# Low halves of the w_out weights by accumulating DMAs instead of VectorE subtractions

## The chip, the cores and the metric

The kernel runs on one core of one Trainium2 chip. The metric is the device time of one execution in microseconds (us), lower is better. The core's engines are named as the profile names them: PE (TensorE, matmuls), DVE (VectorE), ACT (ScalarE), POOL (GpSimd) and SP (SyncE, which here only issues DMAs). The engines run their own instruction queues in order and wait for each other by semaphores; 16 DMA engines move the data of all queues.

## What is computed

One decoder layer for 512 positions and a model width of 2048. A conditioning vector c gives shift, scale and gate by an adaLN product; h is x scaled and shifted; one input product makes q, k, v, two gates and the two halves of a GLU; the attention branch (sliding window, 16 heads) and the convolution branch (depthwise convolution, layer norm, pointwise product) make 1024 channels each; the output product w_out mixes both, and a layer norm over the residual ends it.

```python
mod = (c_act @ w_ada[l] + b_ada[l])[:, None, :]
shift, scale, gate = jnp.split(mod, 3, axis=-1)
h = x * (1.0 + scale) + shift
proj = h @ w_in[l]
...
y_attn = banded_sink_attention(q, k, v, rel_bias, sinks[l]) * jax.nn.silu(g_attn)
y_conv = conformer_conv(...) * jax.nn.silu(g_conv)
y = jnp.concatenate([y_attn, y_conv], axis=-1) @ w_out[l]
x = layer_norm(ALPHA * x + gate * y, ln_g[l], ln_b[l])
```

## The kernel before

Every product is made of three passes on PE. Each float32 operand is split into a high half (rounded to the matmul's input format, `fp32r`) and a low half (what the rounding left), and `mm3` sums high x high, low x high and high x low in PSUM. For weights the split is made on the fly: `load_w` loads a block of 128 x 1024 values (512 KB) into a tile `wr`, ACT copies it into `wh` (the rounding, line 174), and DVE subtracts `wh` from `wr` into `wl` (line 175). The tiles `wr`, `wh` and `wl` have three buffers each.

The work runs in phases: (1) h and the GLU projections; (2) q, k, v, gate and attention, with the depthwise convolution as filling work on DVE; (3) the convolution's gate; (4) from about 545 to 632 us, the output product over the attention channels: 4 column groups n of 4 blocks of w_out, kp = 0 to 3, 24 matmuls a block (4 position tiles x 2 chunks x 3 passes); (5) the pointwise product w_pw, 8 blocks; (6) the output product over the convolution's channels, kp = 4 to 7. In phase 6 the column groups n = 0 and 1 take 8 blocks of w_out through `wh` and `wl` as in phase 4; the 8 blocks of n = 2 and 3 (the "late" blocks, `late_block`) are split meanwhile into the space of h (`hh`, `hl`), and a last product over them follows, one position tile after the other, with the layer norm behind each. The raw tiles of both kinds are the three buffers of `wr`.

Phase 4 has filling work on DVE: `gate_steps` streams the gate's part of w_ada through two buffers `wa` (32 half rows of 512 KB) and reduces each against the activations of c (`junk`, line 588). Its result is needed for the residual in phase 5.

The program's text gives what depends on what; the order within each engine's queue is set by a scheduler that places instructions by a model of their durations. A change of one instruction's kind can so move others.

Names used below: `wr`, `wh`, `wl` raw, high and low weights; `hh`, `hl` high and low halves of h, later of the attention's and the convolution's channels and of the late weights; `ych`, `ycl` the halves of the convolution branch; `prj`, `att` the two sets of PSUM tiles; `xs` tiles of x for the residual; `lg`, `lb` the layer norm's parameters; `z` the residual sum.

Of the kernel before, what the change touches and what calls it, by code (L numbers as in the profile page):

```python
# [10 lines left out]
F32 = mybir.dt.float32  # L11
# [33 lines left out]

# smalls: columns of one [128, n] array
SM_ADA = 0
# [6 lines left out]

# the first phase goes over the contraction chunks as they come; these pairs of
# output tiles (glu_a, glu_b) stay in PSUM, the others are summed part by part.
N_FIXED = 3
# [3 lines left out]

# microseconds of other work for the vector engine with each block of weights
N_WARM = 5
# [11 lines left out]
def plan():  # L75
    """The order of the first phase: the next chunk of h, unless the tensor engine would wait for weights."""
    done = {i: 0 for i in range(N_FIXED, NC8)}
    items, fixed, n_h = [("h", 0)], 0, 1
    dma, pe = 8.5, 11.0
    while n_h < NK:  # L80
        item = None
        i = min(done, key=lambda j: (done[j], j))
        n = min(n_h - done[i], PART[1])
        if pe - dma < LEAD:
            if fixed < n_h:
                item, dma, pe = ("fix", fixed), dma + 1.1, max(pe, dma + 2) + 3.9
                fixed += 1
            elif n >= min(PART[0], n_h):
                item, dma, pe = ("rot", i, done[i], n), dma + 0.37 * n, max(pe, dma + 2) + 1.3 * n
                done[i] += n  # L90
        if item is None:
            item, dma = ("h", n_h), dma + 6.6
            n_h += 1
        items.append(item)
    items += [("fix", k) for k in range(fixed, NK)]
    # what is left of each pair, most of it first
    rest = sorted(done, key=lambda j: (done[j], j))
    return items + [("rot", i, done[i], NK - done[i]) for i in rest if done[i] < NK]


def parts_of(k0, n):
    """At most four chunks to a block."""
    m = -(-n // 4)
    cuts = [k0 + n * a // m for a in range(m + 1)]
    return list(zip(cuts[:-1], cuts[1:]))


def w_in_blocks():
    """The blocks of w_in in the order of use: (first chunk, chunks, columns)."""
    blocks = []  # L110
    for item in plan():
        if item[0] == "fix":
            blocks.append((item, item[1], 1, [c for i in range(N_FIXED) for c in ab_cols(i)]))
        elif item[0] == "rot":
            for ka, kb in parts_of(*item[2:]):
                blocks.append((("rot", item[1], ka), ka, kb - ka, ab_cols(item[1])))
    for c in [C_K, C_V] + [x + 256 * j for j in range(NKV) for x in (0, C_GA)] + [C_GC + 256 * j for j in range(4)]:
        for k in range(0, NK, 4):
            blocks.append((("col", c, k), k, 4, [(c, 256)]))
    return blocks  # L120


def bucket_runs():
    """(bucket, first distance, one past the last distance) for distances 0..127."""
    max_exact = N_BUCKETS // 2
    runs = []
    for d in range(P):
        if d < max_exact:
            b = d
        else:  # L130
            big = np.log(np.float32(d) / np.float32(max_exact)) / np.float32(math.log(MAX_DISTANCE / max_exact))
            b = min(max_exact + int(np.float32(big * np.float32(N_BUCKETS - max_exact))), N_BUCKETS - 1)
        if runs and runs[-1][0] == b:
            runs[-1][2] = d + 1
        else:
            runs.append([b, d, d + 1])
    return runs


def build(tc, xT, x, c, wadaT, smalls, win, wpw, wout, relT, sinks, ln_g, ln_b, out):  # L140
# [11 lines left out]

    # ---- the activations of c, on all partitions
    ones = pp.tile([P, P], F32, name="ones")
# [17 lines left out]
    def split(raw, hi, lo, hi_engine=None):  # L172
        """hi + lo = raw, each with 12 significant bits."""
        nc.scalar.activation(hi, raw, AF.Copy)  # L174
        nc.vector.tensor_tensor(lo, raw, hi.bitcast(F32), op=ALU.subtract)  # L175
# [15 lines left out]
    def silu_c(pool, psp, tag):  # L191
        # the products of ones that come first set the tensor engine's clock
        warm = psp.tile([P, S], F32, name="warm", tag=tag)
# [5 lines left out]
        parts = [slice(i * S, (i + 1) * S) for i in range(4)]  # L199
        # the halves of c lie where the last chunks of h come later  # L200
        chl = [(hh[0:1, NK - 4 + i, :], hl[0:1, NK - 4 + i, :]) for i in range(4)]
# [12 lines left out]
    def ada(pool, cb, js, parts=1):  # L214
        """columns js of mod: for each, 128 outputs of the adaLN product, one per partition."""
        wa = [pool.tile([P, D], F32, name="wa", bufs=WA_BUFS) for j in js]
# [9 lines left out]

    # ---- phase 1: h and the GLU projections, chunk by chunk
    glu = {}
# [55 lines left out]
    def conv_steps():  # L284
        """the depthwise convolution, two chains at a time"""
        for i0 in range(0, NC8, 2):
# [14 lines left out]
    def take(gen, budget):  # L301
        """some of the work that fills the vector engine between the splits of the weights"""
        while budget > 0:
            cost = next(gen, None)
            if cost is None:
                return
            budget -= cost
# [9 lines left out]

    # ---- phase 2: q, k, v, the gate, and attention
    def chain(*gens):
# [10 lines left out]

    # the negated bias of each head over the distance + 128; elsewhere the mask
    rel = p2.tile([16, N_BUCKETS], F32, name="rel", bufs=1)
# [58 lines left out]
    def attention(j, qs, sg, nb, n):  # L391
        """a block of queries of four heads, in three stages"""
        blk = slice(n * P, (n + 1) * P)
# [6 lines left out]
        def scores():  # L400
            # the negated scores, and after them the negated sink
            e = kept["e"] = p2.tile([P, GRP, 2 * P + 1], F32, name="e")
# [36 lines left out]
        def values():  # L439
            pv = ps2.tile([P, S], F32, name="att", bufs=5)  # L440
            for half, (pth, ptl) in enumerate(kept["p"]):
# [3 lines left out]
                nc.tensor.matmul(pv[:HD, :], v[:, 0, :], ptl, start=False, stop=half == nh - 1, skip_group_check=True)  # L445
            # the products with the low halves of the values lie in the upper partitions
            low = p2.tile([HD, S], F32, name="low", bufs=1)
# [9 lines left out]

    # the stages of attention go between the products of the next projections
    stages = {}
# [7 lines left out]
    for j in range(NKV):  # L467
# [14 lines left out]
        nb = p2.tile([P, GRP, 256], F32, name="nb")  # L482
        # [query, head, 255 - key]
        nc.sync.dma_start(nb, bass.AP(tensor=ext_d.tensor, offset=ext_d.offset + GRP * j * 384 + 1,
# [7 lines left out]

    # ---- phase 3: the gate of the convolution, and its layer norm
    def gc_out(j):
# [26 lines left out]
    def norm_steps():  # L521
# [27 lines left out]
        ps = colsum(tot)  # L549
        # 1 / sqrt(var + eps), and one Newton step: r (1.5 - 0.5 v r^2)  # L550
        nc.scalar.activation(tot, ps, AF.Sqrt, bias=eps, scale=1.0 / D_CONV)
# [12 lines left out]
        yield None  # L564
        # the normalised channels, through silu, take the place of the last chunks of h
        for i in range(NC8):
# [33 lines left out]
    def y_split(k0):  # L600
        # y of attention takes the place of the first chunks of h
        if k0 < 8:
            for k in range(k0, k0 + 4):
                split(y[:, k, :], hh[:, k, :], hl[:, k, :])
# [5 lines left out]

    # ---- phase 4: the output product over the channels of attention
    def w_out_block(n, kp):
        return load_w(wout, (n * 8 + kp) * P * 1024, 1024)

# [20 lines left out]

    # ---- phase 5: the pointwise product, its bias and gate; the attention half so far into the residual
    p5 = es.enter_context(tc.tile_pool(name="p5", bufs=1, reuse_waits="tile"))
# [56 lines left out]

    # ---- phase 6: the output product over the channels of the convolution, and the last layer norm
    def yh(k):
# [12 lines left out]

    # the weights of the last two column groups take the place of h  # L710
    def late_block(n, kp):
# [3 lines left out]
        ks = slice((n - 2) * 8 + 2 * (kp - 4), (n - 2) * 8 + 2 * (kp - 4) + 2)  # L715
        split(raw.rearrange("p (a b) -> p a b", a=2), hh[:, ks, :], hl[:, ks, :])

# [13 lines left out]
    for t in range(NB):  # L731
        ts_ = slice(t * P, (t + 1) * P)
        for n in (2, 3):
            # the last product in two parts, for what follows it to start early
            parts = [slice(0, HALF), slice(HALF, S)] if (t, n) == (NB - 1, 3) else [slice(0, S)]
# [21 lines left out]
def laid_out(x, c, w_ada, b_ada, w_in, rel_bias, sinks, conv_w, conv_b, conv_ln_g, conv_ln_b, w_pw, b_pw, w_out,  # L757
             ln_g, ln_b):
    x, w_in = np.asarray(x)[0], np.asarray(w_in)[0]
    cols = lambda v, n: np.asarray(v)[0].reshape(n, P).T  # noqa: E731  # L760
    cw = np.asarray(conv_w)[0].T.reshape(NC8, P, TAPS).transpose(1, 0, 2).reshape(P, NC8 * TAPS)
# [31 lines left out]
```

## Time and profile before

| | |
|---|---|
| median of 3 runs | 790.63 us (789.19 to 792.8) |
| span of the profiled execution | 788.9 us |
| PE busy | 760.9 us, 96% |
| DVE busy | 676.0 us, 86% |
| ACT busy | 341.8 us, 43% |
| POOL busy | 20.5 us, 3% |
| 512 KB loads of w_out | 32, median 4.6 us from issue to landing |

The profile is of one execution. A busy PE is the sum of its matmuls' records; the records overlap, so that the distance from one matmul's start to the next tells the pace. The time before the first and after the last recorded instruction is not in the span; beside the median of the runs it is 1.7 us.

### The profile page before, as it was taken

How to read it: one execution, taken by the hardware profiler on the slowest of the kernel's cores; microseconds unless marked ns; L12 is line 12 of the kernel's file. 1: busy time of each engine (PE TensorE's matmuls, PEld its weight loads, DVE VectorE, ACT ScalarE, POOL GpSimd, SP SyncE). 2: the span in 40 equal slices, each digit the busy share in tenths (PEclk: the TensorE clock that was granted, in tenths of full speed). 3: DMA queues.
4: the chain of work that ended last, by engine and by line, in shares of the span. 5: the costliest groups of instructions: out<-in, count | busy, mean ns of one | idle time of the engine just before them, and what ended most of it. 6: DMA issues, size and time to landing. Idle time of an engine off the chain costs nothing.

```text
span 788.9 us, 9718 instructions
## 1 busy us (share of the span) xinstructions
PE 760.9 (96%) x3522; PEld 628.9 (80%) x3522; DVE 676.0 (86%) x1101; ACT 341.8 (43%) x574; POOL 20.5 (3%) x30
## 2 busy tenths in 40 slices
PE   5999999999999999999999999999999799999994
PEld 4787888878898888888888888888878588888883
DVE  6888988959999999999999998579795539877797
ACT  4543333333242346656756756445473145433000
POOL 0000000000230000000000100000000000000000
PEclk9999999999999999999999999999999989999997
DMA  8999988513332232322321322367667633684033
GB/s 308 414 412 410 359 324 308 185 60 109 114 134 101 86 104 95 107 67 78 107 81 54 106 81 81 102 225 222 239 215 243 221 134 123 224 302 152 0 107 107
DMA packets 39089, 136.10 MB, mean 173 GB/s; under 512 B 4337, under 2 KB 6785, under 8 KB 34817
## 3 DMA queue, kind: packets, MB, share of 16 engines
q1 hardware_dynamic: 39042, 135.49, 49.2%
q8 instruction: 27, 0.44, 0.2%
q14 instruction: 20, 0.16, 0.1%
HBM read 131.26 MB, written 4.22 MB: 172 GB/s over the span
## 4 chain that ended last, share of the span: by engine, by line
PE 80%; DVE 9%; DMA 7%; issue 2%; ACT 0%; SPq 0%; DVEq 0%
PE prj L187 14%; PE prj L188 14%; PE prj L189 14%; DMA wa<-in_wadaT 6%; PE rot L187 5%; PE rot L189 5%; PE rot L188 5%; PE att L188 4%; PE att L189 4%; PE att L187 4%; PE fix L187 3%; DVE junk L588 3%; PE fix L188 3%; PE fix L189 3%; PE att L433 2%
## 5 line engine op out<-in xcount | busy, mean ns | idle before, releaser
L174 ACT ACTIVATE wh<-wr 128x1024 fp32r<-128x1024 f32 (+2 forms) x129 | 127.3, 997 | 203.5 <-PE prj L188 109.7
L187 PE MATMUL prj<-hh,wh 128*128 128x512 f32 x480 | 188.5, 393 | 0.0
L189 PE MATMUL prj<-hh,wl 128*128 128x512 f32 x480 | 187.6, 392 | 0.0
L188 PE MATMUL prj<-hl,wh 128*128 128x512 f32 x480 | 187.5, 391 | 0.0
L175 DVE TENSOR_TENSOR wl<-wr,wh 128x1024 fp32r<-128x1024 f32 (+2 forms) x129 | 147.3, 1145 | 27.5 <-ACT wh L174 27.1
L295 DVE SCALAR_TENSOR_TENSOR cv<-u,sm,cv 128x512 f32<-128x512 f32 x240 | 169.5, 743 | 0.8
L189 PEld LDWEIGHTS prj<-hh,wl 128*128 128x128 f32 x480 | 90.2, 188 | 19.4 <-issue 0.2
L187 PEld LDWEIGHTS prj<-hh,wh 128*128 128x128 f32 x480 | 90.2, 188 | 18.8 <-issue 0.2
L188 PEld LDWEIGHTS prj<-hl,wh 128*128 128x128 f32 x480 | 90.3, 188 | 18.1
L224 DVE CUSTOM_DVE_ANT_0 junk<-wa,cb,sm 128x2048 bf16<-128x2048 f32 (+1 forms) x32 | 72.9, 2279 | 2.6 <-DMA wa<-in_wadaT 2.6
L187 PE MATMUL rot<-hh,wh 128*128 128x512 f32 x160 | 62.2, 393 | 1.7 <-DVE acc L272 1.7
L188 PE MATMUL rot<-hl,wh 128*128 128x512 f32 x160 | 62.6, 391 | 0.0
L189 PE MATMUL rot<-hh,wl 128*128 128x512 f32 x160 | 62.5, 392 | 0.0
L188 PE MATMUL att<-wl,hh 128*128 128x512 f32 (+1 forms) x144 | 50.9, 354 | 6.7 <-DVE wl L175 6.7
L189 PE MATMUL att<-wh,hl 128*128 128x512 f32 (+1 forms) x144 | 50.2, 349 | 0.0
L187 PE MATMUL att<-wh,hh 128*128 128x512 f32 (+1 forms) x144 | 48.5, 349 | 0.0
L188 PE MATMUL fix<-hl,wh 128*128 128x512 f32 x96 | 38.2, 398 | 0.0
L187 PEld LDWEIGHTS rot<-hh,wh 128*128 128x128 f32 x160 | 30.3, 189 | 9.5 <-DVE acc L272 1.7
L189 PE MATMUL fix<-hh,wl 128*128 128x512 f32 x96 | 37.8, 394 | 0.0
L188 PEld LDWEIGHTS att<-wl,hh 128*128 128x128 f32 x144 | 28.0, 194 | 11.9 <-DVE wl L175 8.6
L189 PEld LDWEIGHTS rot<-hh,wl 128*128 128x128 f32 x160 | 30.1, 188 | 6.8 <-DVE wl L175 0.3
L188 PEld LDWEIGHTS rot<-hl,wh 128*128 128x128 f32 x160 | 30.1, 188 | 6.4
(163 smaller groups left out, 1179.3 us busy)
## 6 DMA issues: line engine op xcount, KB each, us to landing
wr<-in_win SPq DMA_DIRECT2D x68, 512.0 KB, 3.4
wa<-in_wadaT SPq DMA_DIRECT2D x30, 1024.0 KB, 8.6
wa<-in_wadaT SPq DMA_DIRECT2D x36, 512.0 KB, 5.0
wr<-in_wout SPq DMA_DIRECT2D x32, 512.0 KB, 4.6
wr<-in_win SPq DMA_DIRECT2D x24, 384.0 KB, 9.0
xt<-in_xT SPq DMA_DIRECT2D x16, 256.0 KB, 9.1
wr<-in_wpw SPq DMA_DIRECT2D x8, 512.0 KB, 3.3
xs<-in_x SPq DMA_DIRECT2D x16, 256.0 KB, 5.2
```

What stands on the lines that cost most here:

```text
L174: nc.scalar.activation(hi, raw, AF.Copy)
L175: nc.vector.tensor_tensor(lo, raw, hi.bitcast(F32), op=ALU.subtract)
L187: nc.tensor.matmul(ps, lh, rh, start=start, stop=False)
L188: nc.tensor.matmul(ps, lh, rl, start=False, stop=False)
L189: nc.tensor.matmul(ps, ll, rh, start=False, stop=stop)
L224: nc.vector.tensor_tensor_reduce(junk[:, part], w[:, part], cb[:, part], 1.0, first, ALU.mult, ALU.add, mod[:, j:j + 1])
L295: nc.vector.scalar_tensor_tensor(cv[i][:, :S], glu[i][:, j:j + S], w, cv[i][:, :S], op0=ALU.mult, op1=ALU.add)
L433: nc.tensor.transpose(pt[:, hd * P:(hd + 1) * P], kept["e"][:, hd, half * P:(half + 1) * P], ident)
L588: nc.vector.tensor_tensor_reduce(junk, wa, cb[:, hs], 1.0, dst if half else first, ALU.mult, ALU.add, dst)
```

## The change

The low half of a w_out block is no longer a DVE subtraction. ACT writes the negated high half into the low tile (a copy with scale -1, rounded as the high half is), and then a DMA issued from POOL with `accum_op=add` adds the raw weights to it in place: -hi + raw. ACT writes the high half by a copy of its own as before. For the 16 blocks of phase 4 (kp < 4) the DMA reads the weights in HBM a second time, for the 16 blocks of phase 6 it reads the tile `wr`. The splits of w_in, w_pw and of activations are as they were. The diff also drops comments, which moves line numbers.

```diff
+    def add_raw(lo, src):
+
+        nc.gpsimd.dma_start(lo, src, accum_op=ALU.add)
+
     def w_out_block(n, kp):
-        return load_w(wout, (n * 8 + kp) * P * 1024, 1024)
+        src = wout[(n * 8 + kp) * P * 1024:][:P * 1024].rearrange("(p e) -> p e", p=P)
+        raw = wp.tile([P, 1024], F32, name="wr")
+        nc.sync.dma_start(raw, src)
+        hi = wp.tile([P, 1024], F32R, name="wh")
+        lo = wp.tile([P, 1024], F32R, name="wl")
+        nc.scalar.activation(lo, raw, AF.Copy, scale=-1.0)
+        add_raw(lo, src if kp < 4 else raw)
+        nc.scalar.activation(hi, raw, AF.Copy)
+        return hi, lo
...
     def late_block(n, kp):
         raw = wp.tile([P, 1024], F32, name="wr")
         off = (n * 8 + kp) * P * 1024
         nc.sync.dma_start(raw, wout[off:off + P * 1024].rearrange("(p e) -> p e", p=P))
         ks = slice((n - 2) * 8 + 2 * (kp - 4), (n - 2) * 8 + 2 * (kp - 4) + 2)
-        split(raw.rearrange("p (a b) -> p a b", a=2), hh[:, ks, :], hl[:, ks, :])
+        raw2 = raw.rearrange("p (a b) -> p a b", a=2)
+        nc.scalar.activation(hl[:, ks, :], raw2, AF.Copy, scale=-1.0)
+        add_raw(hl[:, ks, :], raw2)
+        nc.scalar.activation(hh[:, ks, :], raw2, AF.Copy)
```

The order of the queues changes with it, at three places that matter below. The first is DVE at the end of phase 4, before; `junk_5340`, `junk_5344` and `junk_5348` are the last three of the 32 half reductions, `wl_5241` and `wl_5279` the low halves of the last two w_out blocks, `wl_5364` and `wl_5417` those of the first two w_pw blocks.

```order
L588 ISA junk_5340,mod_65<-wa_5338,cb_4869,mod_65 128x1024
L588 ISA mod_65 128x1
L588 ISA junk_5344,mod_65<-wa_5342,cb_4869,sm_64 128x1024
L588 ISA mod_65 128x1
L175 TENSOR_TENSOR wl_5241<-wr_5238,wh_5240 128x1024
L588 ISA junk_5348,mod_65<-wa_5346,cb_4869,mod_65 128x1024
L588 ISA mod_65 128x1
L656 SCALAR_TENSOR_TENSOR dl_5393<-ident_70,mod_65,dh_5392 128x128 x4
L175 TENSOR_TENSOR wl_5279<-wr_5276,wh_5278 128x1024
L175 TENSOR_TENSOR wl_5364<-wr_5361,wh_5363 128x1024
L175 TENSOR_TENSOR wl_5417<-wr_5414,wh_5416 128x1024
```

The same place of DVE with the change; here `junk_5356`, `junk_5360` and `junk_5364` are the last three half reductions, `wl_5380` and `wl_5433` the low halves of the first two w_pw blocks.

```order
L588 ISA junk_5356,mod_65<-wa_5354,cb_4874,mod_65 128x1024
L588 ISA mod_65 128x1
L175 TENSOR_TENSOR wl_5380<-wr_5377,wh_5379 128x1024
L588 ISA junk_5360,mod_65<-wa_5358,cb_4874,sm_64 128x1024
L588 ISA mod_65 128x1
L588 ISA junk_5364,mod_65<-wa_5362,cb_4874,mod_65 128x1024
L588 ISA mod_65 128x1
L175 TENSOR_TENSOR wl_5433<-wr_5430,wh_5432 128x1024
```

The w_out splits are gone from between the reductions, and the first split of w_pw now stands ahead of the last two reductions, behind thirty.

The second place is SP in phase 6, before: the loads of the raw tiles and of x around the middle of the phase (`wr` of line 714 is a late block, of line 180 one that is used at once).

```order
L714 DMA wr<-in_wout 128x1024
L180 DMA wr<-in_wout 128x1024
L714 DMA wr<-in_wout 128x1024
L180 DMA wr<-in_wout 128x1024
L666 DMA xs<-in_x 128x512 x2
L693 DMA lb<-in_ln_b 128x2048
L666 DMA xs<-in_x 128x512 x8
L714 DMA wr<-in_wout 128x1024
```

The same place of SP with the change (late blocks at line 726, the others at line 619).

```order
L726 DMA wr<-in_wout 128x1024
L619 DMA wr<-in_wout 128x1024
L678 DMA xs<-in_x 128x512 x2
L705 DMA lb<-in_ln_b 128x2048
L678 DMA xs<-in_x 128x512 x7
L726 DMA wr<-in_wout 128x1024
L619 DMA wr<-in_wout 128x1024
L678 DMA xs<-in_x 128x512
```

The batch of x loads moves ahead of the third late block and the fourth of the others, which now wait for adds: each load of a raw tile into a buffer waits for the add that reads the buffer's former contents.

The third place is PE in phase 6 with the change, at the sixth block that is used at once (`wh_5989`, `wl_5990`); `att_6115` is a PSUM tile of the last product, `hh_71` and `hl_72` hold the late weights.

```order
L187 MATMUL att_5950<-wh_5989,ych_5371 128x512
L187 MATMUL att_6115<-hh_71,ych_5371 128x512
L188 MATMUL att_6115<-hl_72,ych_5371 128x512
L189 MATMUL att_6115<-hh_71,ycl_5372 128x512
L187 MATMUL att_6115<-hh_71,ych_5371 128x512
L188 MATMUL att_6115<-hl_72,ych_5371 128x512
L189 MATMUL att_6115<-hh_71,ycl_5372 128x512
L187 MATMUL att_6115<-hh_71,ych_5371 128x512
L188 MATMUL att_6115<-hl_72,ych_5371 128x512
L189 MATMUL att_6115<-hh_71,ycl_5372 128x512
L187 MATMUL att_6115<-hh_71,ych_5371 128x512
L188 MATMUL att_6115<-hl_72,ych_5371 128x512
```

Eleven matmuls of the last product stand there ahead of the first one that reads `wl_5990`; at the fifth, seventh and eighth of these blocks it is three each. Before, none of the last product's matmuls stood among these blocks.

## Rows read from the trace of the kernel before

**Rows 1.** The page: busy time by engine, and the clock granted in 40 slices.

```profile
PE 760.9 (96%) x3522; PEld 628.9 (80%) x3522; DVE 676.0 (86%) x1101; ACT 341.8 (43%) x574; POOL 20.5 (3%) x30
PE   5999999999999999999999999999999799999994
PEclk9999999999999999999999999999999989999997
```

**Rows 2.** Stretches: PE, PEld, DVE, ACT, POOL busy; clock; DMA share; GB/s.

```profile
0.00:100.00 100.00, 91.38 (x376) 72.32 (x376) 83.13 (x103) 44.92 (x64) 1.16 (x14) 1.00 0.98 381
545.00:632.00 87.00, 80.26 (x347) 64.59 (x346) 64.19 (x88) 33.98 (x45) 0.00 (x0) 0.99 0.68 230
645.00:688.00 43.00, 43.00 (x190) 35.32 (x189) 35.26 (x56) 19.73 (x33) 0.00 (x0) 1.00 0.48 159
688.00:732.00 44.00, 44.00 (x196) 36.48 (x195) 33.33 (x48) 15.07 (x15) 0.00 (x0) 1.00 0.64 215
```

**Rows 3.** Waits from 515 to 640 us: us in total, times, longest.

```profile
PE att L188 <- DVE wl L175: 6.7, 4, 4.2
```

**Rows 4.** The chain in order of time: start, us, what.

```profile
595.71 7.46 DMA wa<-in_wadaT
...
623.01 5.33 DMA wa<-in_wadaT
```

**Rows 5.** DVE in order of time: the 30th and the 32nd half reduction.

```profile
625.94 1.28 DVE L588 CUSTOM_DVE_ANT_0 junk<-wa,cb,mod 128x1024 bf16<-128x1024 f32 x1 [2.96 <-DMA wa<-in_wadaT]
...
631.02 1.28 DVE L588 CUSTOM_DVE_ANT_0 junk<-wa,cb,mod 128x1024 bf16<-128x1024 f32 x1
```

**Rows 6.** PE in order of time: start, us, what, idle before and who ended it.

```profile
621.06 0.50 PE L188 MATMUL att<-wl,hh 128*128 128x512 f32 x1 [1.02 <-DVE wl L175]
...
630.96 0.80 PE L188 MATMUL att<-wl,hh 128*128 128x512 f32 x1 [4.16 <-DVE wl L175]
631.55 0.63 PE L189 MATMUL att<-wh,hl 128*128 128x512 f32 x1
631.98 0.63 PE L187 MATMUL att<-wh,hh 128*128 128x512 f32 x1
...
644.35 0.39 PE L187 MATMUL prj<-hh,wh 128*128 128x512 f32 x1
```

**Rows 7.** A stretch behind the longest wait, columns as in rows 2.

```profile
631.00:636.20 5.20, 5.20 (x12) 4.09 (x13) 4.12 (x8) 3.17 (x6) 0.00 (x0) 0.50 0.30 104
```

**Rows 8.** Groups by form from 500 us on: busy us, mean ns; idle before, releasers.

```profile
L175 DVE TENSOR_TENSOR wl<-wr,wh 128x1024 fp32r<-128x1024 f32 x38 | 46.4, 1222 | 20.0 <-ACT wh L174 19.9
L174 ACT ACTIVATE wh<-wr 128x1024 fp32r<-128x1024 f32 x37 | 38.9, 1056 | 53.6 <-PE att L189 20.3 <-PE prj L188 19.6 <-DMA wr<-in_wout 5.7
```

**Rows 9.** DMA issues: count, KB each, median us to landing.

```profile
wa<-in_wadaT SPq DMA_DIRECT2D x30, 1024.0 KB, 8.6
...
out<-z SPq DMA_DIRECT2D x16, 256.0 KB, 2.8
...
lg<-in_ln_g SPq DMA_DIRECT2D x1, 1024.0 KB, 4.8
```

**Rows 10.** The loads of w_out issued from 695 to 730 us.

```profile
DMA to landing us min/median/max: 3.2/4.2/6.5
```

**Rows 11.** SP in order of time: issues in phases 5 and 6.

```profile
666.79 0.33 SPq L180 DMA_DIRECT2D wr<-in_wout  x1
...
672.65 0.33 SPq L714 DMA_DIRECT2D wr<-in_wout  x1
...
689.80 0.90 SPq L666 DMA_DIRECT2D xs<-in_x  x2
...
699.99 0.33 SPq L714 DMA_DIRECT2D wr<-in_wout  x1
```

**Rows 12.** ACT in order of time: the first late block's copy.

```profile
677.89 1.06 ACT L174 ACTIVATE hh<-wr 128x1024 fp32r<-128x1024 f32 x1 [3.18 <-DMA wr<-in_wout]
```

**Rows 13.** PE in order of time: the first matmul of phase 6's first block.

```profile
690.03 0.39 PE L187 MATMUL prj<-wh,ych 128*128 128x512 f32 x1
```

## The prediction

> **What bounds the kernel now.** I read the page's busy shares and slices first [rows 1]: TensorE (PE) is busy 96% of the span, at a full granted clock except in one slice two thirds of the way in, and there its busy share drops as well. VectorE (DVE) stands at 86%. So a cut of VectorE's work is worth only what PE waits for VectorE. The stages, read as stretches [rows 2], narrow it: from 545 to 632 us (the output product over the attention channels, 16 blocks of w_out) PE is idle 6.7 of 87 us; in the pointwise product (645 to 688) and the output product's second half (688 to 732) PE is full. The waits say who ended that idle time [rows 3]: PE waited for the subtraction of line 175, 6.7 us in 4 waits, the longest 4.2 us.
>
> Why was the subtraction late? From 595 us on the chain in order of time goes through loads of w_ada (tile wa) [rows 4] and the VectorE reductions on them (junk, line 588): VectorE waits for such a load, 2.96 us before the thirtieth reduction [rows 5], and the next block's subtraction is queued behind it. PE's rows show the price [rows 6]: idle 4.16 us until 630.96, and then matmuls that start 0.43 us apart instead of 0.23. The granted clock there is 0.50, the lower level (1.2 of 2.4 GHz), for 12 matmuls [rows 7]. A wait of 1.02 us at 621.06 was followed by the usual pace [rows 6].
>
> **What the change removes.** 32 subtractions of 1.22 us [rows 8], 39 us of VectorE. Nearly all lie beside PE work; what is on the path is the 6.7 us of waits and 12 matmuls at 0.20 us too much, 2.4 us. Term 1: -9.1 us. The subtraction no longer stands behind the reductions, so nothing of this wait is left in that form. Next late there is the first split of w_pw, which stays on VectorE: the order shows it behind 30 of the 32 half reductions, and the second one behind all. Before, the reductions were through at about 632 us, the thirtieth near 627 [rows 5]. With term 1, PE wants w_pw at about 644.3 - 9.1 = 635 us [rows 6]. So the w_ada stream may come some 6 us later before it costs anything, and its loads share the transfer engines with the new adds. It keeps two loads in flight; the chain has five waits for them from 595.71 to 623.01 [rows 4], so a pair takes 27.3 / 4 = 6.8 us; of the pairs, some ten run beside the adds. Half a microsecond more for each is 5 us, covered; one microsecond is 10 us, 4 uncovered. Term 2: between 0 and +4, I take +2.
>
> **What it adds.** On ScalarE 32 negated copies, 1.06 us each [rows 8], 34 us; it is busy 34 of 87 us in the first stage and 15 of 44 in the other [rows 2], so they fit, but one stands in each block's path and is counted below. On GpSimd's queue 32 adding DMAs; GpSimd does nothing else from 545 us on (0.00 in those stretches of rows 2), so each waits only for those ahead of it. For 16 blocks the add reads w_out from HBM again (8.4 MB), for the other 16 it reads the raw tile.
>
> The price of one add, A, from the copy's end to the moment that its waiters go on, is in no row. Bounds by the nearest: below, the 256 KB stores, 2.8 us [rows 9], and the shortest 512 KB load of that stretch, 3.2 [rows 10]; above, the 1,024 KB loads, 4.8 us in a quiet stretch (lg) and 8.6 in the crowded first 100 us (wa) [rows 9]. An add has to read the old contents as well as the source, two times 512 KB, so the nearest row is the 1,024 KB load of lg; with a little for neighbours I take A = 5.0. The Trainium skill, "Collectives: The Full Stack", section "The bandwidth ceiling: the fold count and why AG ≠ RS ≠ AR", says the same of a reducing transfer: the addition itself is free, but two source reads pass one read ring, and the rate halves. Another page of the Trainium skill speaks for less: "DMA: Bandwidth & Descriptors", section "Anatomy of one DMA — SWDGE (gpsimd) path", gives 2.0 us + bytes / 436e3 per microsecond for a transfer issued by GpSimd, an estimate of 3.2 us for 512 KB, with which term 3 below would be 4.0 us; no row here shows either.
>
> In the first stage A hardly shows. A low half can be rewritten when the block three before it is done, and is wanted two blocks later: 2 x 24 matmuls x 0.226 = 10.8 us (43 us / 190 matmuls [rows 2]), against 1.1 + A and some ScalarE work. It decides from about A = 9.
>
> In the second stage the raw tile is held until its add is done, where the subtraction gave it back after 1.06 + 1.22 us; and 16 loads (8 blocks used at once, 8 "late" ones kept for the last product) go through 3 raw buffers. The order of SP shows which load waits for what. In times of the trace of before: the first block's raw load is issued at 666.79, the first late one's at 672.65 [rows 11]; its copy starts at 677.89 [rows 12]. Four ScalarE copies take both to about 682.2; the first block's add ends at 682.2 + A. The load of the third block waits for that. Behind it SP has nine loads of x and the one of lb; ten and lb took 10.2 us before (689.80 to 699.99 [rows 11]), which I carry: 692.4 + A. Then come, by buffers given back in turn, the third late load, the fifth block, the sixth late load and the eighth block, four links of issue 0.33 + landing 4.2 (the median of that stretch [rows 10]) + copy 1.06 + 0.3 of hand-over + A = 5.9 + A. The eighth block is ready at 692.4 + A + 4 (5.9 + A) = 716.0 + 5A. PE wants it at 690.03 + 7 x 24 x 0.226 = 728.0 [rows 2, 13]. Lateness: 5A - 12.0. Term 3: A = 5.0 gives +13.0; A = 2.8 gives +2.0, A = 8.6 gives +31.0.
>
> Term 4: the order of PE shows about 20 matmuls of the last product drawn forward into the gaps between these blocks. They are work done in the wait: 20 x 0.226 = -4.5 us (nothing, if their own late weights are late).
>
> Term 5: the lateness comes in several waits, of which I expect two as long as the one of 4.16 us; by its price in slow matmuls, 2 x 2.4 = +4.8 us (0 if none is that long, 4 of them 9.6).
>
> The last product, the layer norm and the stores after the last matmul keep their order and cost.
>
> **Sum.** -9.1 + 2 + 13.0 - 4.5 + 4.8 = +6.2 us on a span of 788.9, that is 795.1. The median of the three runs shown is 790.63, 1.7 above the profiled span, and I carry that: 797 us.
>
> **Rivals.**
> Quick adds, on the other side: an add lands like a plain 512 KB load, A near 3.2. Then term 3 is 4.0, less than the matmuls drawn forward, no wait is long, and only term 1 is left: 788.9 - 9.1 + 1.7 = 781.5 us. For it speaks that the raw loads land in 3.2 us at best in just that stretch, and that the second 16 adds touch no HBM; against it that the median there is 4.2 [rows 10] and the add reads twice as much. It decides as long as A is under about 4.
> The two cancel: A near 4.0. Term 3 is +8.0, less 4.5, one long wait +2.4, term 2 +2, term 1 -9.1: -1.2, 789 us.
> The transfers fill up: in the first stage 230 GB/s are moved at a share of 0.68 [rows 2], 20.0 MB. The 16 adds there read 16.8 MB; 36.8 MB at the 389 GB/s of the first 100 us (381 at a share of 0.98 [rows 2]) take 94.6 us, 14 more than the 80.3 that PE needs. Then w_ada and w_pw come late, and in the second stage A is rather 7: term 3 +23.0, less 4.5, three long waits +7.2, term 1 -9.1, +14: +31, 821 us. Against it: if an add loads the engines like a plain copy, half of that is gone.
> That the change doesn't do what it says (subtractions left on VectorE in these stages) is excluded by the order of VectorE: none of tile wr from w_out is left.
>
> **How the numbers follow.** Forecast (A of 4.4 to 6.5) 0.42; quick adds 0.28; cancelling 0.13; full transfers 0.17. About 4 us, 0.5%, is what a measurement of this kernel tells from no change. Slower: 0.17 and most of the forecast's 0.42, less what of it lies under +4 us (0.04): 0.55. Same: 0.13 and that 0.04: 0.17. Faster: 0.28. The range goes from the quick case to the full one, 781 to 821; outside are a still lower end and A over 7. The forecast's own range is 791 to 808.
>
> **What would show it.** Term 1: no PE wait for line 175 between 545 and 632, and the slow matmuls after 631 gone. Term 2: the first w_pw split right behind a reduction that waits for wa, with PE idle there. A: time from a negated copy to the go of what waits for the add, and the time to landing of the new DMAs. Term 3: PE waiting for adds from the fourth block of the second stage on, more with each third block, and SP's raw loads waiting for the adds. If PE waits nowhere after 688, quick adds are right; if SP's loads in the first stage land in 7 us and more and PE waits there, the full transfers are. The forecast is wrong if A is under 4 us, or if the raw buffers turn out not to be what the second stage waits for.

## The result and the profile after

The changed kernel takes 822.09 us (median of 4 runs, 821.59 to 823.44), the kernel before 789.91 beside it: 1.0407 times as long, 95% interval 1.0383 to 1.0431, or 32 us more. The forecast was 797 us, the range 781 to 821. The sign was right, the size was not, and the time lies just past the upper end. The profiled execution has a span of 820.8 us, 31.9 more than the one of before.

First the page, with the rows that answer to [rows 1]: busy time by engine, then PE, its granted clock and the share of the DMA engines in 40 slices, and two queues: packets, MB, share of 16 engines' span (q0 holds the 32 adds, q1 all loads and stores).

```profile
PE 771.2 (94%) x3522; PEld 633.0 (77%) x3522; DVE 640.3 (78%) x1069; ACT 369.8 (45%) x606; POOL 48.5 (6%) x62
PE   6999999999999999999999999989999899758994
PEclk9999999999999999999999999989999999888997
DMA  8999988223423322223123223799999748999233
q1 hardware_dynamic: 39042, 135.49, 46.8%
q0 software_dynamic: 4608, 16.78, 11.1%
```

VectorE is relieved as meant (676.0 to 640.3 us), and PE's lowest slice between its two ends, the 32nd before [rows 1], is now the 36th. The row to look at is DMA: from the 26th slice (513 us) on it stands at 7 to 9, but for one slice in phase 5, up to the 37th. The queue rows give the price of an add in the time of the engines: 11.1% of 820.8 us / 32 = 2.85 us of all 16 engines, where 512 KB of the other queue took 46.8% of 820.8 / 258 = 1.49 us (135.49 MB are 258 times 512 KB).

The two halves of the output product as stretches, before and then after (columns as in [rows 2]).

```profile
545.00:645.00 100.00, 93.26 (x394) 75.14 (x393) 69.31 (x96) 40.46 (x56) 0.00 (x0) 0.97 0.66 221
690.00:770.00 80.00, 80.00 (x354) 66.31 (x353) 62.27 (x103) 15.32 (x17) 0.00 (x0) 1.00 0.41 139
```

```profile
545.00:645.00 100.00, 92.32 (x388) 73.94 (x387) 44.01 (x66) 48.74 (x62) 12.19 (x14) 0.97 0.98 278
690.00:770.00 80.00, 61.60 (x236) 47.89 (x235) 22.23 (x40) 29.64 (x31) 12.16 (x14) 0.87 0.92 232
```

In the first half the engines go from a share of 0.66 to 0.98; they move 278 GB/s there, where 381 went at the same share in the first 100 us [rows 2]. In the second half it is 0.41 x 80 = 33 us of engine time before and 0.92 x 80 = 74 after; the difference, 41 us, is the 14 adds issued there at 2.85 us (40), and the 7.4 MB that are moved in addition are their bytes, so the loads beside them are no more than before. PE was full there before and has 61.60 of 80 us now.

PE's waits from 540 to 800 us (us in total, times, longest), the five largest:

```profile
PE prj L188 <- DMA wl<-wr: 9.4, 2, 5.6
PE att L188 <- DMA wl<-wr: 5.5, 3, 2.9
PE prj L188 <- DMA wl<-in_wout: 4.9, 2, 3.8
PE att L188 <- DMA wl<-in_wout: 2.8, 3, 1.6
PE prj L187 <- ACT wh L624: 2.4, 1, 2.4
```

Of [rows 3], 6.7 us for line 175, nothing is left in the first half; 7.7 us for adds that read HBM have come in its place, and 14.9 us for adds that read the raw tile in the second half. In PE's order of time (start, us, what, idle before and releaser) the phases begin and the long waits lie here:

```profile
550.09 0.80 PE L188 MATMUL prj<-wl,hh 128*128 128x512 f32 x1 [3.79 <-DMA wl<-in_wout]
...
645.90 0.39 PE L187 MATMUL prj<-hh,wh 128*128 128x512 f32 x1
...
694.96 0.39 PE L187 MATMUL prj<-wh,ych 128*128 128x512 f32 x1
...
712.51 0.80 PE L188 MATMUL prj<-wl,ych 128*128 128x512 f32 x1 [5.60 <-DMA wl<-wr]
...
726.50 0.80 PE L188 MATMUL prj<-wl,ych 128*128 128x512 f32 x1 [3.76 <-DMA wl<-wr]
...
754.67 0.79 PE L188 MATMUL att<-wl,ych 128*128 128x512 f32 x1 [2.92 <-DMA wl<-wr]
...
765.28 0.50 PE L188 MATMUL att<-wl,ych 128*128 128x512 f32 x1 [1.38 <-DMA wl<-wr]
```

Phase 5 starts at 645.90 (before 644.35 [rows 6]): the gain of term 1 is eaten up, and 1.6 us more. Phase 6 starts at 694.96 (690.03 [rows 13]), so phase 5 lost 3.4. From there to the end it is 125.8 us, where it was 98.9: 27.0. Behind the long waits the granted clock is low for all or part of 5 us, as in [rows 7] (columns as there; 0.50 is the lower level, what lies between is a mean of both, and a share above 1 in so short a stretch is read here as full):

```profile
550.00:555.30 5.30, 5.21 (x12) 4.13 (x13) 0.37 (x1) 0.00 (x0) 0.00 (x0) 0.50 1.05 301
712.50:717.70 5.20, 5.19 (x15) 4.17 (x16) 4.04 (x6) 0.12 (x1) 0.00 (x0) 0.63 1.05 410
726.50:731.60 5.10, 5.10 (x15) 4.13 (x16) 2.49 (x5) 0.30 (x1) 0.00 (x0) 0.66 1.02 279
754.70:759.90 5.20, 5.20 (x12) 4.10 (x13) 0.00 (x0) 0.64 (x1) 0.00 (x0) 0.50 0.87 245
```

The DMA issues of phase 6 (count, KB each, median us to landing), from 695 to 735 us of the trace before, and from 695 to 765 us of the one after:

```profile
wr<-in_wout SPq DMA_DIRECT2D x9, 512.0 KB, 4.2
xs<-in_x SPq DMA_DIRECT2D x3, 256.0 KB, 8.5
```

```profile
wr<-in_wout SPq DMA_DIRECT2D x12, 512.0 KB, 7.0
hl<-wr POOLq DMA_DIRECT2D x7, 512.0 KB, 5.9
wl<-wr POOLq DMA_DIRECT2D x6, 512.0 KB, 6.0
xs<-in_x SPq DMA_DIRECT2D x10, 256.0 KB, 12.9
```

Adds land in 6 us, which is not far from the 5.0 taken for A; but the plain loads beside them go from 4.2 to 7.0. That a neighbour slows down points to a full resource; a chain of latencies alone would leave the loads at their pace. SP's issues (start, us), which answer to [rows 11]: the first load, then the batch of x and the loads behind it up to that of the eighth block.

```profile
672.32 0.33 SPq L619 DMA_DIRECT2D wr<-in_wout  x1
...
698.37 5.36 SPq L678 DMA_DIRECT2D xs<-in_x  x7
708.14 0.33 SPq L726 DMA_DIRECT2D wr<-in_wout  x1
711.32 0.33 SPq L619 DMA_DIRECT2D wr<-in_wout  x1
...
752.21 0.33 SPq L619 DMA_DIRECT2D wr<-in_wout  x1
```

Over the whole stretch in which the second half's loads and adds run, the engines are busy 0.91 x 93 = 85 us:

```profile
672.00:765.00 93.00, 74.88 (x294) 58.74 (x292) 32.80 (x56) 38.25 (x42) 13.89 (x16) 0.89 0.91 238
```

### The profile page after: what moved, and what is told of

Read it like the earlier page. It is cut to its first block, busy times and chain, and to the rows that moved or that the text cites. A ratio compares the mean times of both kernels' runs of the same rounds, so it can differ in the third digit from the quotient of the medians.

```text
span 820.8 us, 9799 instructions
## 1 busy us (share of the span) xinstructions
PE 771.2 (94%) x3522; PEld 633.0 (77%) x3522; DVE 640.3 (78%) x1069; ACT 369.8 (45%) x606; POOL 48.5 (6%) x62
## 3 DMA queue, kind: packets, MB, share of 16 engines
q1 hardware_dynamic: 39042, 135.49, 46.8%
q0 software_dynamic: 4608, 16.78, 11.1%
## 4 chain that ended last, share of the span: by engine, by line
PE 65%; DMA 21%; DVE 9%; issue 3%; ACT 1%; SPq 1%; DVEq 0%; POOLq 0%; POOL 0%; ACTq 0%
PE prj L189 11%; PE prj L188 11%; PE prj L187 11%; DMA wa<-in_wadaT 11%; PE rot L187 5%; DMA wr<-in_wout 4%; PE rot L189 4%; PE rot L188 4%; PE fix L187 3%; PE fix L188 3%; PE fix L189 3%; DVE junk L588 3%; DMA wl<-wr 2%; PE att L188 2%; PE att L189 2%
## 5 line engine op out<-in xcount | busy, mean ns | idle before, releaser
L174 ACT ACTIVATE wh<-wr 128x1024 fp32r<-128x1024 f32 (+3 forms) x105 | 102.1, 984 | 168.4 <-PE prj L188 100.6
L175 DVE TENSOR_TENSOR wl<-wr,wh 128x1024 fp32r<-128x1024 f32 (+3 forms) x105 | 117.9, 1127 | 17.3 <-ACT wh L174 17.1
L622 ACT ACTIVATE wl<-wr 128x1024 fp32r<-128x1024 f32 x24 | 25.3, 1054 | 49.2 <-DMA wr<-in_wout 41.6
L405 POOL COPY e<-nsink 128x4 f32<-128x4 f32 x16 | 19.4, 1214 | 458.8 <-PE att L433 248.2
L588 DVE CUSTOM_DVE_ANT_0 junk<-wa,cb,sm 128x1024 bf16<-128x1024 f32 x16 | 20.4, 1277 | 33.4 <-DMA wa<-in_wadaT 33.4
L588 DVE CUSTOM_DVE_ANT_0 junk<-wa,cb,mod 128x1024 bf16<-128x1024 f32 x16 | 20.5, 1283 | 29.3 <-DMA wa<-in_wadaT 29.3
```

The costliest lines, as they stand in the source:

```text
L405: nc.gpsimd.tensor_copy(e[:, :, nkeys], nsink[:, heads])
L588: nc.vector.tensor_tensor_reduce(junk, wa, cb[:, hs], 1.0, dst if half else first, ALU.mult, ALU.add, dst)
L622: nc.scalar.activation(lo, raw, AF.Copy, scale=-1.0)
```

## The experiments

The theory with which they began: an add costs the transfer engines about twice a load of its size, so that both halves fill the engines. Rivals: the raw tiles held by the adds (a chain of latencies, term 3 as it was meant), the scheduler's new order, and a fixed price per add (issue, ScalarE's third copy). "kp < 4" below is the first half.

**One half at a time.** In `w_out_block`:

```diff
+        if kp >= 4:                      # e1; e2: if kp < 4
+            return load_w(wout, (n * 8 + kp) * P * 1024, 1024)
```

and in e1 `late_block` with `split` as before.

> Adds only for the 16 blocks of the output product's first half (kp < 4); the second half splits by VectorE subtraction as before. Transfers full (my theory now: an add takes about twice the engine time of a load, 2.85 against 1.49 us of all 16 engines from the queue shares of the changed kernel's page, so that both halves fill the engines): the first half keeps its share near 1.0 and ends about 1.5 us later than before, phase 5 loses 2 to 3 us, the second half loses nothing: 792 to 796 us. Rival, the reordering of queues by the scheduler costs the time wherever adds stand: 800 us and more. Rival, quick adds here and all the loss in the second half: 780 to 783.

> Adds only for the 16 blocks of the second half (kp >= 4, reading the raw tile); the first half as before, with its 6.7 us of waits for line 175. Transfers full: phase 6 is as long as in the changed kernel, 27 us longer than before: 814 to 819. Rival, that the second half starts late and disturbed by the first half's adds (late w_ada, late w_pw): 800 or less.

Measured: e1 796.37 us, 1.0078 (1.0059 to 1.0097), a hair above the 792 to 796 expected; e2 816.64 us, 1.0338 (1.0322 to 1.0354), inside its 814 to 819. The two, 6 and 27 us, add up to the whole. So the second half does not suffer from the first half's adds, and the first half's adds are worth nothing even alone. The adds' queue on the two pages, e1 and then e2 (packets, MB, share):

```profile
q0 software_dynamic: 2304, 8.39, 5.5%
```

```profile
q0 software_dynamic: 2304, 8.39, 5.6%
```

By the spans of 794.1 and 814.1 us that is 2.73 us of the engines for an add that reads HBM, and 2.85 for one that reads the raw tile: the source makes 4% at most.

**Does the held raw tile cost the time?** e3, the adds of the second half from HBM:

```diff
-        add_raw(lo, src if kp < 4 else raw)
+        add_raw(lo, src)
...
-        add_raw(hl[:, ks, :], raw2)
+        add_raw(hl[:, ks, :], wout[off:off + P * 1024].rearrange("(p a b) -> p a b", p=P, a=2))
```

> As the changed kernel, but the adds of the second half read w_out from HBM too, so that a raw tile is given back after ScalarE's two copies and not after the add. The engines have the same adds to make. Transfers full: 812 to 824, as the changed kernel. Rival, the three raw buffers held by the adds (term 3 of the prediction, a chain of latencies): the loads run ahead, the loss of phase 6 goes for the most part: 793 to 800.

Measured 819.72 us, 1.0369 (1.0346 to 1.0392), inside the 812 to 824 of full transfers. Term 3's hold of the raw tiles is gone there, and some 2 us with it (from the start of phase 6 to the end 122.2 us in place of 125.8). It was not what bound the second half.

e10 does the opposite in the first half, `add_raw(lo, raw)` for all blocks:

> As the changed kernel, but the adds of the first half read the raw tile and not HBM a second time. The share of the engines' time per add was the same from either source (2.73 us where all read HBM, 2.85 where all read the tile), so transfers full says no gain: 818 to 826. Rival, the second read of 8.4 MB from HBM makes the first half full: 810 to 816.

Measured 826.84 us, 1.0455 (1.0422 to 1.0488): the rival is out, since 8.4 MB less from HBM bring nothing. The time is 4 to 5 us above the changed kernel's; that this is the hold of the raw tiles is likely, but not shown.

e4 gives the late blocks a raw buffer of their own, `raw = p5.tile([P, 1024], F32, name="lr", bufs=1)`:

> As the changed kernel, but the late blocks' raw loads go through one buffer of their own (a fourth raw buffer), and the order puts five of the eight into phase 5, where the transfer engines stand at a share of 0.57. Transfers full: what is moved out of phase 6 (five loads of 1.49 and adds of 2.85 us of engine time, 22 us) is saved but for what phase 5 lacks: 798 to 806. Rival, the chain through the raw buffers: 795 to 805, not told apart by the time, but by the landing of the adds: 4 to 5 us where the engines are free, against 6.5 and more.

Measured 824.87 us, 1.0432 (1.0404 to 1.0461), against both expectations. With one buffer each late load on SP waits for the add before it (50.6 us in 6 waits from 640 to 765 us), and the loads of w_pw and x behind it on SP wait too: in the profiled run phase 5 takes 5 us more than in the changed kernel, the rest from phase 6 on 7 less. Nothing is won by the earlier place, so this run speaks neither for full transfers nor for the chain. What it does give is the price of an add where the engines have room. From 645 to 690 us of its trace, at a share of about 0.7:

```profile
wr<-in_wpw SPq DMA_DIRECT2D x5, 512.0 KB, 4.8
hl<-lr POOLq DMA_DIRECT2D x4, 512.0 KB, 5.1
```

An add with room around it lands in 5.1 us. The estimate of A was right for that case, and it was the wrong quantity.

**What in the add costs: its addition, or its being there?** e5 leaves every instruction in its place on every queue and takes only the addition away; e6 leaves the additions and takes the bytes:

```diff
-        nc.gpsimd.dma_start(lo, src, accum_op=ALU.add)
+        nc.gpsimd.dma_start(lo, src)                                       # e5
+        nc.gpsimd.dma_start(lo[..., :64], src[..., :64], accum_op=ALU.add) # e6
```

> As the changed kernel with every instruction in its place on every queue, but the 32 DMAs copy the raw weights into the low tile and don't add (so the low halves are not low halves): the same issues, waits and bytes written, without the read of the old contents. Transfers full, because an add reads two sources: a copy costs the engines what a load does, about 1.5 us in place of 2.85, 32 x 1.35 = 43 us of all engines are gone, the landings fall from 6.5 to 9.1 us to 4 to 5, and most of the loss with them: 790 to 800. Rival, that issue and latency of a GpSimd DMA, ScalarE's third copy or the order of the queues cost the time: 815 to 822, as the changed kernel.

> As the changed kernel, but each add moves only the first 64 of a row's 1,024 (late blocks: of 512) values, and the rest of the low half stays unfinished. Issues, waits and ScalarE's copies are there, a sixteenth (late: an eighth) of the bytes; the order differs at some places. Transfers full: the engines are free, an add lands in some 2 to 3 us, and what is left is the gain of the prediction's first term: 780 to 786. Rival, order and ScalarE: 800 and more.

Measured: e5 794.09 us, 1.0056 (1.0036 to 1.0075); e6 792.93 us, 1.0039 (1.0024 to 1.0054). e5 is the decisive run: the same order, issues and bytes written, and 28 of the 32 us are gone. Its queues:

```profile
q1 hardware_dynamic: 39042, 135.49, 48.6%
q0 software_dynamic: 4608, 16.78, 6.0%
```

6.0% of 793.2 us / 32 is 1.49 us for a copy, what a load costs, against 2.85 with the addition: 1.9 times. A copy also lands sooner than an add (medians of 3.7 and 5.7 us in the second half, against 6.6 and 6.5), so e5 alone does not part engine time from latency. Against latency stands e3, where the raw tile no longer waits for the add. PE's first matmuls of phases 5 and 6 in e5:

```profile
637.73 0.39 PE L187 MATMUL prj<-hh,wh 128*128 128x512 f32 x1
...
683.41 0.39 PE L187 MATMUL prj<-wh,ych 128*128 128x512 f32 x1
```

From the second to the end of the span (793.2) it is 109.8 us, where it was 98.9 before and 125.8 with adds: of the 27.0 us lost there the addition is 16.0, and 10.9 are left with copies.

e6 was expected 7 to 13 us quicker; with hardly any bytes the order, the copies and the holds still cost a little more than term 1 brings (106.2 us from the start of phase 6 to the end, 7.3 more than before). So there is a rest beside the engines.

**A half dose, and the rest.** e9 adds only for the late blocks (`late_block` of the change in the kernel before). e13 and e14 are the changed kernel and e5 without most of SP's batch of ten loads (lb and the last eight loads of x are left out; `lg` stands in for lb further down):

```diff
-                xs = small("xs")
-                nc.sync.dma_start(xs[:, :S], x[t * P:(t + 1) * P, cs])
+                xs = small("xs") if n < 2 else gate[:, cs]
+                if n < 2:
+                    nc.sync.dma_start(xs[:, :S], x[t * P:(t + 1) * P, cs])
...
-    nc.sync.dma_start(lb, ln_b.to_broadcast([P, D]))
```

> Adds only for the eight late blocks; the eight blocks of the second half that are used at once, and the first half, by subtraction. Half the dose. Transfers full, with 1.49 us of all engines for a 512 KB load and 2.85 for an add: from the first w_out load of phase 6 (666 us) to the last product (733) the engines have 16 x 1.49 + 8 x 2.85 + 16 x 0.75 of x + 3 of lb = 62 us of work in 67 us, so it just fits, where 16 adds make 85: 790 to 796, far under half of the 27 us. Rival, a price per add (a chain of latencies, issue on POOL, a third copy on ScalarE): half of 27, 801 to 806.

> As the changed kernel, but without the loads of x for two of the four column groups (8 loads of 256 KB; gate stands in for x) and without the load of lb (lg stands in): SP's batch of ten loads in the middle of phase 6 is gone, and the order there is plainly late and used blocks by turns. The output is not the layer's. Transfers full: 9 us of the engines' time are saved (8 x 0.75 + 3) of the 27 lost: 811 to 816. Rival, the place of the batch ahead of the raw loads, in an order that waits for adds, makes most of the loss: 800 and less.

> The same without that batch, with plain copies in place of adds (low halves wrong). If what was left of the loss with copies, some 10 us in phase 6 beside a gain in the first half, is the batch: 783 to 787. If it is the hold of the raw tiles or ScalarE's third copy: 790 to 795.

Measured: e9 799.27 us, 1.0104 (1.0071 to 1.0137), between the two: half the adds cost 9 us and not 13, but the engines' sum said 0 to 6. e13 815.74 us, 1.0320 (1.0291 to 1.0349), as the engines' sum said; the batch makes no large part of the adds' loss. e14 789.20 us, 0.9999 (0.9984 to 1.0014), again between.

Counted from the first w_pw matmul to the end of the span, so without the first half, the kernels take 144.6 us (before), 174.9 (after), 155.5 (e5), 167.5 (e13) and 148.6 (e14). Of the 30.3 us, then, 19.4 are the addition (after less e5); of the 10.9 that are left with copies, 6.9 are the batch (e5 less e14; with adds, after less e13, it is 7.4), and 4.0 remain with neither. The batch's share is its bytes and its place together, which these runs do not part. Each of these is one profiled execution, and executions of one kernel differ by 2 to 5 us here, so the 4.0 are hardly more than noise. Whether they are the hold of the raw tiles, the third copy or the copies' own landings stays open. In e9 PE's longest wait of the second half is for a late block's copy, whose raw load stands behind the batch on SP, as its row in the order of time shows:

```profile
717.38 1.65 PE L187 MATMUL prj<-hh,ych 128*128 128x512 f32 x3 [3.64 <-ACT hh L719]
```

**A version that beats both.** The gain of term 1 needs only the last blocks of the first half to leave VectorE. In the kernel before, the blocks of n = 3 and kp < 4 get these lines, shortened:

```diff
+        nc.scalar.activation(lo, raw, AF.Copy, scale=-1.0)                        # e7
+        nc.gpsimd.dma_start(lo, src, accum_op=ALU.add)
+        nc.scalar.activation(hi, raw, AF.Copy)
...
+        nc.scalar.activation(hi, raw, AF.Copy)                                    # e8
+        nc.gpsimd.tensor_tensor(lo, raw, hi.bitcast(F32), op=ALU.subtract)
```

> Adds for four blocks only, those of the first half's last column group (n = 3, kp < 4), where the kernel before waits for line 175; all other blocks by subtraction. Transfers full: four adds take 4 x 2.85 = 11 us of the engines there, where before a third was idle, so w_ada comes a little later; term 1 is gained for the most part: 781 to 787. Rival, that the wait for the w_ada stream only moves to the first split of w_pw behind it: 788 to 793.

> As the last one, but the four low halves are subtractions on GpSimd, which is idle there, and no DMA is added. If only the place behind the reductions matters: 780 to 785, a little under the four adds. Rival, a GpSimd subtraction of 128 x 1,024 takes over 5 us or slows VectorE down, so that PE waits for it: 790 and more.

Measured: e7 789.19 us, 0.9988 (0.9974 to 1.0002), no change that can be told; e8 785.39 us, 0.9948 (0.9931 to 0.9966), faster than both kernels, than the one before by 4 us. In e7 PE waits once for an add at 632 us, 2.4 us. GpSimd's four subtractions in e8 (POOL by form: busy us, mean ns, idle before):

```profile
L620 POOL TENSOR_TENSOR wl<-wr,wh 128x1024 fp32r<-128x1024 f32 x4 | 9.8, 2451 | 135.6 <-ACT wh L619 135.6
```

More of the same was tried with n >= 2 (e11) and all of kp < 4 (e12):

> The kernel before with the subtractions of the first half's last two column groups (8 blocks) on GpSimd, 2.45 us each as in the run with four. Expected as there or a little better, since another wait for line 175 may go: 783 to 787. Rival, that GpSimd's 2.45 us in place of 1.22 show at each block: 788 to 792.

> The same for all 16 blocks of the first half: no wait for line 175 is left between the reductions. 782 to 786 if the low halves keep up (a block of 24 matmuls is 5.4 us, GpSimd 2.45); rival: the w_ada stream and the first split of w_pw are then what waits, or GpSimd and VectorE slow each other: 788 and more.

Measured: e11 790.10 us, 0.9998 (0.9975 to 1.0020); e12 807.82 us, 1.0211 (1.0178 to 1.0243). Both miss. In e11 the waits for line 175 fall from 6.7 to 1.6 us, but PE then waits for the high half of the first w_pw block:

```profile
640.01 0.80 PE L187 MATMUL prj<-hh,wh 128*128 128x512 f32 x1 [4.54 <-ACT wh L174]
```

In e12 the order makes the largest part. ACT in order of time, and PE behind it:

```profile
643.67 0.98 ACT L663 ACTIVATE dh<-ident,mod 128x128 fp32r<-128x128 f32 x3 [13.94 <-DVE mod L588]
...
645.81 1.99 ACT L619 ACTIVATE wh<-wr 128x1024 fp32r<-128x1024 f32 x2
```

```profile
646.91 0.80 PE L187 MATMUL att<-wh,hh 128*128 128x512 f32 x1 [10.13 <-ACT wh L619]
```

The scheduler put copies for the residual ahead of two blocks' high halves on ACT; they wait 13.94 us for the last w_ada reduction, and PE 10.13 us behind them. GpSimd's pace is the second part: a subtraction takes 2.66 us on average there, and PE waits for it as long in all as it waited for line 175 before (us in total, times, longest):

```profile
PE att L188 <- POOL wl L620: 6.5, 4, 2.1
```

## Why the prediction was wrong, point by point

- **What bounds the kernel** and **term 1** were read rightly in kind: the waits for line 175 are gone with the change. 5.8 of the 6.7 us lie in the last group (0.92 us at 581.32 does not), and e8, which moves only that group's four subtractions, gains 4 us. The whole 9.1 us are seen in no run; the most is the 6.6 us by which phase 5 begins earlier in e5.
- **"In the first stage A hardly shows ... It decides from about A = 9"** is the first step that failed, not by its bound but by the A that was held against it. The adds from HBM had a median of 9.1 us to landing, with the engines at 0.98. New waits of 7.7 us and a slow stretch of 12 matmuls (2.4) took the place of the 9.1 gained; phase 5 began 1.6 us later and not 9.1 less 2 earlier. With copies it began at 637.73, 6.6 earlier: the addition cost 8 us here.
- **Term 2** was +2, at most 4; phase 5 itself lost 3.4, with 1.3 us of wait for the first split of w_pw and the same 1.3 for the residual's small operands. That is right in kind, but that the size fits is luck: the w_ada stream came not 5 to 10 us later but 19 (the thirtieth half reduction starts at 645.31, where it was 625.94 [rows 5]), and it cost so little because PE wanted w_pw only at 645.90 and not at 635.
- **Term 3** is the step that failed in the second half: it was mis-sized, and it took the wrong thing for the limit. It read 5A - 12.0 = 13.0. PE's waits from 694.96 on sum to 18.4 us; with the 4.5 of matmuls drawn forward that is 22.9. The first long wait, 5.60 us, comes at the third block and not from the fourth on. The formula took one A, from loads in a quiet stretch, and left the landing of the raw loads at 4.2 us, as if the adds ran alone. Measured were A = 6.0 and 7.0 for the loads. Four links 2.8 us longer are 11.2, five A 5.0 more, together 16 where 10 would have done. And the chain through the raw buffers was not the bound: without the hold of the raw tiles the time hardly moved (e3), without the addition 16 of the 27.0 us from phase 6 on went (e5). What the term left out is the time of the 16 engines.
- **Term 4** was right: 20 matmuls of the last product stand in the gaps, between 735 and 770 us. **Term 5**, +4.8, was about right in the second half: 15, 15 and 12 matmuls at a granted clock of 0.50 to 0.66 behind the three long waits make some 6 us over the usual pace. 2.6 of the 27.0 us are in none of these.
- **The rival that came true** is the full transfers, with a chance of 0.17. It gave +14 - 9.1 = 4.9 up to phase 6 (measured 4.9) and +25.7 behind it (27.0). Its first part is right in kind: engines full, w_ada late. That its second part comes so near is in part luck, since it goes through term 3 with A = 7, and neither the A (6.0) nor the chain was that. It also holds only for most of the loss: 10.9 us behind the start of phase 6 stay with copies, of which the batch is some 7. The rival was set low on one argument, that an add might load the engines like a copy. That argument decided the case, and e5 shows it false: 2.85 against 1.49 us. The Trainium skill, "Collectives: The Full Stack", section "The bandwidth ceiling: the fold count and why AG ≠ RS ≠ AR", had said of a collective's reduce-scatter that the add needs two source reads and so runs at half the rate; by the ratio of 1.9 the runs agree for the local add here. The prediction used that rule for the latency of one add, and the two reads for a sum over the engines only in this rival's first half. The other rule weighed, of "DMA: Bandwidth & Descriptors" in the Trainium skill, section "Anatomy of one DMA — SWDGE (gpsimd) path", makes an estimate of 3.2 us for 512 KB; no add of 512 KB here landed under 4.5, while the late blocks' plain copies in e5 took 3.7 (median of 8).
- **The step to do otherwise**: the engines' sum for phase 6 by rows at hand. 16 loads and 16 adds that count as two are 48 times 512 KB, with the batch of x and lb some 29 MB; at the 389 GB/s of its own rival that is 74 us, where from the first load (666.79 [rows 11]) to the point at which PE wants the eighth block (728) there are 61. The 13 us too many are no more than term 3 had, but they name the right limit. With the engine times measured since, and with all 14 loads of x, lg and lb, it is 16 x 1.49 + 16 x 2.85 + 14 x 0.75 + 2 x 3 = 86 us (the trace has 85), 25 too many, against the 22.9 measured. The prediction made this sum for the first half, as a rival, and not for the second.

## What to carry to other kernels

Before work is moved to DMAs, add up the transfer engines' time of the stage, with an accumulating DMA as two transfers, and set it beside the stage's length: a latency estimate of one transfer, however good, says nothing once that sum is near it. An engine that looks idle all through (GpSimd here) may do the few instructions that are on the path better than the DMA queues (e8 against e7); and only those few should be moved, since each changed instruction lets the scheduler rearrange queues that were in balance (e11, e12).

## What the runs showed of the hardware

- An accumulating DMA takes 1.8 to 1.9 times the engine time of a copy of the same bytes (1.49 us for 512 KB), from HBM (2.73) as from SBUF (2.85). Its issue on POOL is longer as well. POOL by form (busy us, mean ns, idle before), with the adds and with copies (e5):

```profile
L614 POOL DMA_DIRECT2D wl<-wr x8 | 7.0, 871 | 34.5 <-ACT wl L622 22.7 <-DMA wr<-in_wout 11.8
```

```profile
L614 POOL DMA_DIRECT2D wl<-wr x8 | 4.2, 528 | 27.6 <-ACT wl L622 26.2 <-DMA wr<-in_wout 1.4
```

- That is 871 ns against 528: with the addition the issue takes 0.34 us longer. It is part of each add's way, but small beside the landing of 6 us.
- A subtraction of 128 x 1,024 takes 2.45 us on GpSimd in e8 (2.66 in e12, where sixteen are there), twice the 1.22 of VectorE [rows 8].
